# A decode-step kernel on one core: value products of two heads behind two transposes

## The chip, the cores and the metric

The kernel runs on one core of a Trainium2 chip. The metric is the device time of one execution in microseconds (us), lower is better. Engines are named as in the profile: PE (matrix products), PEld (PE's weight loads), DVE, ACT, POOL and SP; SP and POOL also issue DMAs.

## The reference, cut to what matters

One layer mixes two groups of heads over 512 prompt tokens and 32 sampled tokens: an RWKV-7 recurrence and a sparse attention with three branches (compressed, selected, sliding window). The change touches only the prompt's selected and window branches, which here are both full causal attention over the 512 tokens: a query may choose 16 blocks of 64 and there are only 8, and the window is 512 long.

```python
def masked_softmax(s, mask):
    s = jnp.where(mask, s.astype(jnp.float32), MASK_NEG)
    p = jax.nn.softmax(s, axis=-1)
    return jnp.where(mask, p, 0.0)

def window_attn(q, kw, qpos, kpos):
    mask = (kpos[None, :] <= qpos[:, None]) & (kpos[None, :] > qpos[:, None] - WINDOW) & (kpos[None, :] >= 0)
    s = jnp.einsum('bkgtd,bskd->bkgts', q, kw[:, :, 0]) * ATTN_SCALE
    p = masked_softmax(s, mask)
    return jnp.einsum('bkgts,bskd->bkgtd', p.astype(q.dtype), kw[:, :, 1])

# mixer_out: the three branches are weighted with sigmoid gates and added
    o = g[0] * o_c + g[1] * o_s + g[2] * o_w
```

There are 8 query heads, written as 4 groups g of 2 key/value heads k, each 64 wide.

## The kernel before, in words

The kernel has four stages: the input projection (to about 340 us), then the recurrence of the prompt interleaved with the prompt's attention (about 340 to 535 us), then the sampled tokens' attention over the paged cache together with the prompt's output projection, then a short end.

**The attention.** `attention()` goes through four token tiles i of 128 queries. For each tile it runs one unit `compressed(i)` and eight units `full(i, br, g)`, for 2 branches br and 4 groups g. A unit of `full` does, for both k: scores (L1231, L1232, and the causal mask L1233) into a PSUM bank of `SBANK`, the row maximum on DVE (L1234), the exponential with its sum on ACT (L1235) into `pr`; then the weights are scaled on DVE by gate over sum (L1237 to L1244). The weights lie with queries on partitions, so they are transposed on PE (L1250) into a bank of `PBANK`, two key tiles and both k at once, a *part* of up to four 128x128 transposes. The part is copied to the SBUF tile `ps` (L1252 on DVE or L114 on ACT), and the value products (L1256) add `VP` times `ps` into the accumulator bank `OT`. A value product has 64 output rows: k=0 fills partitions 0 to 63, k=1 fills 64 to 127. The trace shows each such fp32 product as two records of 128x64 weights.

**Banks.** PSUM has eight banks. `PBANK` is the single bank `bn[2]` (bn_3254 in the order of instructions) until the recurrence is over; then `bt[0]` (bt_67) is added. `SBANK` is `bn[0]`, `bn[1]`, and later also the two `ba` banks. `ps` has two buffers.

**What sets the order.** `attention()` is a generator. The first yields of a unit (the scores) run, then up to `BK_` = 2 yields of the unit before it (transposes, value products) come between. The recurrence's generator paces the whole: each of its steps yields a number, and the attention is advanced until its own yields add up to it. That is only the order in which the program states the instructions. The framework's scheduler then orders every engine's instructions itself from the dependences, and takes an instruction ahead of an earlier one that is not yet ready in its own estimate. Each engine executes its list in order. From the third stage on the order is kept as written.

Of the kernel before, what the change touches and what calls it, by code (L numbers as in the profile page):

```python
# [7 lines left out]
F32 = mybir.dt.float32  # L8
# [3 lines left out]
AF = mybir.ActivationFunctionType  # L12
OP = mybir.AluOpType
AX = mybir.AxisListType
PSUM = bass.MemoryType.PSUM

P = 128
# [30 lines left out]
PRE = 'dd'  # L48
# [10 lines left out]
def tile_hymba_step(  # L59
# [8 lines left out]
    nc = tc.nc  # L68
# [6 lines left out]
    small = ctx.enter_context(tc.tile_pool(name="small", bufs=4))  # L75
# [8 lines left out]
    def nxt(n, banks):  # L84
        turn[n] = (turn[n] + 1) % len(banks)
        return banks[turn[n]]
# [14 lines left out]
    mm = nc.tensor.matmul  # L101
    tp = nc.tensor.transpose
    act = nc.scalar.activation
    tt = nc.vector.tensor_tensor
    ts = nc.vector.tensor_scalar
    stt = nc.vector.scalar_tensor_tensor
    red = nc.vector.tensor_reduce
    cp = nc.vector.tensor_copy
# [4 lines left out]
    def acopy(o, i, scale=1.0):  # L113
        return act(o, i, AF.Copy, scale=scale)  # L114
# [8 lines left out]
    VP = vp.tile([P, 2, 4, P], F32, name="VP")  # L123
    gpt = vp.tile([P, 4, 24], F32, name="gpt")
# [83 lines left out]
    ident = ct([P, P], name="ident")  # L208
    ts(ident, jp, 0.0, None, op0=OP.is_equal)
    identb = ct([P, P], BF, name="identb")  # L210
    cp(identb, ident)
    causb = ct([P, P], BF, name="causb")
# [258 lines left out]
    for p in range(4):  # L471
# [49 lines left out]
        for c in range(NCH):  # L521
            tok = slice(c * C, c * C + C)
# [14 lines left out]
    for u in range(4):  # L537
        n = min(4, 13 - 4 * u)
# [25 lines left out]
    for s in range(31):  # L564
        n, m = s + 1, 31 - s
# [113 lines left out]
    qstk = QR.rearrange("p (k g n) -> p k g n", k=2, g=4)  # L679
    kdh = WR[:, 2048:4096].rearrange("p (b k n) -> p b k n", b=2, k=2)  # L680
    kdl = WR[:, 0:2048].rearrange("p (b k n) -> p b k n", b=2, k=2)
# [253 lines left out]
    at = pool(cs_, "at", 2)  # L935
# [245 lines left out]
    SBANK = [bn[0], bn[1]]  # L1181
    PBANK = [[bn[2], bt[1]], [bn[2]], [bn[2], bt[1]], [bn[2], bt[0]], [bn[2], bn[2], bt[0]]][NBK]
    OT = ob_.rearrange("p (g q) -> p g q", g=4)
# [33 lines left out]
                   skip_group_check=True)  # L1217
        yield 860

    def full(i, br, g):  # L1220


        n = (i + 1) * P
        nq = max(n, 256)
        tok = slice(i * P, n)
        l2 = small.tile([P, 2], F32, name="lb")
        nm = small.tile([P, 2], F32, name="nm")
        pr = at.tile([P, 2, NPR], F32, name="pr", bufs=NPRB)
        for k in range(2):
            S = nxt("s", SBANK)  # L1230
            mm(S[:, 0:nq], qstk[:, k, g, tok], kdh[:, br, k, 0:nq], start=True, stop=False)  # L1231
            mm(S[:, 0:nq], qstk[:, k, g, tok], kdl[:, br, k, 0:nq], start=False, stop=False)  # L1232
            mm(S[:, i * P:n], identb, causb, start=False, stop=True)  # L1233
            red(nm[:, k:k + 1], S[:, 0:n], axis=AX.X, op=OP.max, negate=True)  # L1234
            act(pr[:, k, 0:n], S[:, 0:n], AF.Exp, bias=nm[:, k:k + 1], accum_out=l2[:, k:k + 1])  # L1235
            yield 165 * (i + 1)
        nc.vector.reciprocal(l2, l2)  # L1237
        tt(l2, l2, gpt[:, i, 8 + 8 * br + g:16 + 8 * br:4], op=OP.mult)
        for k in range(2):
            e = PRE[k]  # L1240
            if e == "a":
                acopy(pr[:, k, 0:n], pr[:, k, 0:n], l2[:, k:k + 1])
            else:
                (nc.gpsimd if e == "p" else nc.vector).tensor_scalar(pr[:, k, 0:n], pr[:, k, 0:n], l2[:, k:k + 1], None, op0=OP.mult)  # L1244
        for t0 in range(0, i + 1, 2):
            nt = min(2, i + 1 - t0)
            pT = nxt("p", PBANK)
            for t in range(nt):
                for k in range(2):
                    tp(pT[:, (2 * t + k) * P:(2 * t + k + 1) * P], pr[:, k, (t0 + t) * P:(t0 + t + 1) * P], ident)  # L1250
            ps = at.tile([P, 512], F32, name="ps", bufs=2)
            (acopy if (g + t0 // 2) % 2 else cp)(ps[:, 0:2 * nt * P], pT[:, 0:2 * nt * P])  # L1252
            yield 220 * nt
            for t in range(nt):
                for k in range(2):
                    mm(OT[64 * k:64 * k + 64, g, :], VP[:, br, t0 + t, 64 * k:64 * k + 64],  # L1256
                       ps[:, (2 * t + k) * P:(2 * t + k + 1) * P], start=False,
                       stop=(br == 1 and t0 + t == i), skip_group_check=True)
            yield 150 * nt
        if g == 3 and br == 1:  # L1260
            tt(G[:, 4:8, tok], OT, G[:, 4:8, tok], op=OP.mult)

    def attention():
        units = []
        for i in range(4):
            units.append((compressed(i), 1))
            units += [(full(i, br, g), 2) for br in range(2) for g in range(4)]
        late, back = [], iter(())
        for u, n in units:
            for _ in range(n):  # L1270
                yield next(u)
                for _ in range(BK_):
                    y = next(back, None)
                    if y is not None:
                        yield y
            late.append(u)
            if len(late) > LAG:
                yield from back
                back = late.pop(0)
        for u in [back] + late:  # L1280
            yield from u

    A = attention()
    t = 0
    def side():
# [427 lines left out]
    with tc.manual_schedule(engines={ET.PE, ET.DVE, ET.Activation, ET.Pool}):  # L1713
        for s in range(8 * B):
            b, i = divmod(s, 8)
# [91 lines left out]
```

## Time and profile before

| what | us |
|---|---|
| median of 3 runs | 806.1 (802.2 to 810.11) |
| the profiled execution | 805.09 |
| its span (first to last instruction) | 803.3 |
| PE busy | 719.6 |
| DVE busy | 515.4 |
| ACT busy | 341.8 |
| value products, 320 records on PE | 27.4 |

Busy PE is not PE at its peak: a record's duration contains the time to drain, and the next product starts before it ends. What a product costs is read from the distance between starts.

### The profile page before, as it was taken

How to read it: one execution, taken by the hardware profiler on the slowest of the kernel's cores; microseconds unless marked ns; L12 is line 12 of the kernel's file. 1: busy time of each engine (PE TensorE's matmuls, PEld its weight loads, DVE VectorE, ACT ScalarE, POOL GpSimd, SP SyncE). 2: the span in 40 equal slices, each digit the busy share in tenths (PEclk: the TensorE clock that was granted, in tenths of full speed). 3: DMA queues.
4: the chain of work that ended last, by engine and by line, in shares of the span. 5: the costliest groups of instructions: out<-in, count | busy, mean ns of one | idle time of the engine just before them, and what ended most of it. 6: DMA issues, size and time to landing. Idle time of an engine off the chain costs nothing.

```text
span 803.3 us, 17119 instructions
## 1 busy us (share of the span) xinstructions
PE 719.6 (90%) x6922; PEld 602.2 (75%) x6922; DVE 515.4 (64%) x1236; ACT 341.8 (43%) x731; POOL 293.5 (37%) x323
## 2 busy tenths in 40 slices
PE   3997988998899999699999999988989999998775
PEld 2896977888787999598888787665757766676553
DVE  7687587779921520867766665855776666667653
ACT  5335635542021223234544343455554664656420
POOL 5276566554231164500011023224443554434100
PEclk9998998999799899769999999999999999999977
DMA  7733233265373133311115100389888889898841
GB/s 212 264 90 99 63 95 95 53 169 111 81 157 88 29 105 79 119 21 27 28 27 133 27 8 1 127 294 369 301 326 286 304 321 312 299 344 321 253 126 60
DMA packets 103912, 125.01 MB, mean 156 GB/s; under 512 B 59085, under 2 KB 90551, under 8 KB 95386
## 3 DMA queue, kind: packets, MB, share of 16 engines
q1 hardware_dynamic: 94074, 56.48, 26.4%
q0 software_dynamic: 9216, 67.11, 23.0%
q8 instruction: 54, 0.88, 0.4%
q10 hardware_dynamic: 544, 0.33, 0.2%
q14 instruction: 24, 0.20, 0.1%
HBM read 112.81 MB, written 15.26 MB: 159 GB/s over the span
## 4 chain that ended last, share of the span: by engine, by line
PE 61%; DVE 18%; DMA 10%; issue 5%; ACT 4%; POOL 2%; SPq 1%; POOLq 0%; DVEq 0%; ACTq 0%
PE bx L366 16%; DMA pg<-in_cache_kv_dram,idx 5%; PE bn L1256 2%; PE bn L1571 2%; PE ba L1391 2%; PE bt L1001 2%; PE bn L1250 2%; PE bt L1398 2%; PE bn L1519 2%; PE bn L1504 2%; PE bt L1009 1%; DVE LT L566 1%; PE bn L1231 1%; DVE CHL L1565 1%; PE bt L1381 1%
## 5 line engine op out<-in xcount | busy, mean ns | idle before, releaser
L366 PE MATMUL bx<-xh,WR 128*128 128x272 f32 x992 | 182.9, 300 | 2.6 <-POOL WR L360 2.3
L366 PEld LDWEIGHTS bx<-xh,WR 128*128 128x128 f32 x992 | 149.7, 197 | 6.2 <-POOL WR L360 2.7
L366 PE MATMUL bx<-xl,WR 128*128 128x272 f32 x496 | 110.5, 299 | 0.0
L1332 POOL DMA_INDIRECT pg<-in_cache_kv_dram,idx x64 | 62.6, 978 | 119.1 <-PE bn L1530 18.3
L360 POOL TENSOR_TENSOR WR<-WA,WR 128x1024 fp32r<-128x1024 f32 x31 | 76.1, 2454 | 70.5 <-ACT WR L114 70.3
L366 PEld LDWEIGHTS bx<-xl,WR 128*128 128x128 f32 x496 | 83.3, 198 | 0.9
L1571 PE MATMUL bn<-WHL,CHL 128*128 128x256 f32 x384 | 64.8, 304 | 3.9 <-DVE CHL L1565 2.6
L1571 PEld LDWEIGHTS bn<-WHL,CHL 128*128 128x128 f32 x384 | 51.7, 195 | 8.6 <-DVE CHL L1565 4.3
L114 ACT ACTIVATE WR<-WA 128x1024 fp32r<-128x1024 f32 x31 | 32.7, 1056 | 57.6 <-PE bx L366 26.7
L1382 DVE COPY ktc<-bt 128x512 f32<-128x512 f32 x38 | 26.1, 687 | 32.4 <-PE bt L1381 32.4
L1025 POOL TENSOR_TENSOR std<-st,DC 128x512 f32<-128x512 f32 x7 | 7.3, 1049 | 99.5 <-DVE st L1051 37.6
L1565 DVE TENSOR_TENSOR CHL<-G,CHL 128x256 fp32r<-128x256 f32 x64 | 32.2, 503 | 17.1 <-ACT CHL L114 17.1
L1235 ACT ACTIVATE pr<-bn,nm 128x128 f32<-128x128 f32 (+3 forms) x57 | 28.8, 507 | 26.1 <-PE bn L1250 12.1
L1391 PE MATMUL ba<-ktc,WA 128*32 128x255 f32 x512 | 34.0, 383 | 6.3 <-DVE ktc L1382 4.7
L114 ACT ACTIVATE kts<-bt 128x512 f32<-128x512 f32 x43 | 25.5, 593 | 31.1 <-PE bt L1398 31.1
L1234 DVE TENSOR_REDUCE nm<-bn 128x1 f32<-128x128 f32 (+3 forms) x57 | 26.0, 461 | 7.1 <-PE bn L1233 6.7
L1555 POOL TENSOR_TENSOR WHL<-WA,WHL 128x512 fp32r<-128x512 f32 x16 | 21.1, 1338 | 25.7 <-ACT WHL L114 25.7
L1398 PEld LDWEIGHTS bt<-ident,pg 128*128 128x128 f32 x172 | 18.6, 140 | 15.0 <-issue 10.0
L114 ACT ACTIVATE vt<-pg 128x1024 f32<-128x1024 f32 x28 | 29.4, 1048 | 0.0
L1398 PE MATMUL bt<-ident,pg 128*128 128x128 f32 x172 | 27.4, 282 | 2.1 <-DMA pg<-in_cache_kv_dram,idx 2.0
L1256 PE MATMUL bn<-ps,VP 128*64 128x128 f32 x320 | 27.4, 287 | 1.2 <-ACT ps L114 1.0
L1391 PEld LDWEIGHTS ba<-ktc,WA 128*32 128x32 f32 x512 | 14.3, 109 | 18.0 <-DVE ktc L1382 5.2
(544 smaller groups left out, 1774.7 us busy)
## 6 DMA issues: line engine op xcount, KB each, us to landing
WA<-in_w_in_dram SPq DMA_DIRECT2D x23, 512.0 KB
WA<-in_w_in_dram SPq DMA_DIRECT2D x16, 256.0 KB
vt<-in_cache_kv_win_dram SPq DMA_DIRECT2D x8, 512.0 KB
out_dram<-in_cache_kv_win_dram SPq DMA_DIRECT2D x8, 508.0 KB
bkd<-bkv SPq DMA_DIRECT2D x4, 816.0 KB
bd<-bkd SPq DMA_DIRECT2D x16, 192.0 KB
xt<-in_x_prompt_dram SPq DMA_DIRECT2D x4, 512.0 KB
WA<-in_w_out_dram SPq DMA_DIRECT2D x4, 512.0 KB
```

The lines of the kernel that those rows point to most:

```text
L114: return act(o, i, AF.Copy, scale=scale)
L360: ptt(lo[:, :, :n], src[:, :, :n], h[:, :, :n], op=OP.subtract)
L366: mm(z[:, u, 0:HT], w[:, t, :], x[u][:, t, :], start=first, stop=last)
L1234: red(nm[:, k:k + 1], S[:, 0:n], axis=AX.X, op=OP.max, negate=True)
L1235: act(pr[:, k, 0:n], S[:, 0:n], AF.Exp, bias=nm[:, k:k + 1], accum_out=l2[:, k:k + 1])
L1256: mm(OT[64 * k:64 * k + 64, g, :], VP[:, br, t0 + t, 64 * k:64 * k + 64], ps[:, (2 * t + k) * P:(2 * t + k + 1) * P], start=False, stop=(b ...
L1332: nc.gpsimd.indirect_dma_start(out=t, out_offset=None, in_=cache_rows, in_offset=bass.IndirectOffsetOnAxis(ap=idx[:, 2 * b + c_t:2 * b + c ...
L1382: (acopy if i == 3 and b else cp)(KCT[b, q][:, :, c_t, :], pt.rearrange("p (t c) -> p t c", t=4))
L1391: mm(SCB[r, 0:255], QW[:, 4 * q + t, m, :], kt[:, t].rearrange("p a c -> p (a c)")[:, m:m + 255], start=(q == 0 and t < 2), stop=(q == 3 a ...
L1398: tp(pt[:, t * P:(t + 1) * P], PG[b, i][:, t, 2, :], ident)
L1565: tt(CHL[c][:, 1], cat, CHL[c][:, 0], op=OP.subtract)
L1571: mm(YB[:, 0:256], CHL[c][:, x, t], WHL[:, w, 2 * c + t], start=(c + t + x + w == 0), stop=(c + t == 2 and w == 1))
```

## The change: what it does, and the diff

`full` now takes a tuple of groups `gs`. In the first two token tiles a unit handles two groups, (0, 1) or (2, 3); both lie in one `pr` buffer, 256 columns each. In the last two tiles a unit still has one group, which has two parts. In every tile the unit now states all its transposes and copies first and all its value products after them, with one yield for the products instead of one for each part. `ps` has four buffers instead of two. The engine of the copy is chosen by `u + t0 // 2` instead of `g + t0 // 2`. The number of arithmetic operations and their shapes stay as they were.

```diff
-    def full(i, br, g):
+    def full(i, br, gs):
...
+        for u, g in enumerate(gs):
...
+            w = slice(256 * u, 256 * u + n)
...
-        for t0 in range(0, i + 1, 2):
+        parts = [(u, t0) for u in range(len(gs)) for t0 in range(0, i + 1, 2)]
+        made = []
+        for u, t0 in parts:
             nt = min(2, i + 1 - t0)
             pT = nxt("p", PBANK)
             for t in range(nt):
                 for k in range(2):
-                    tp(pT[:, (2 * t + k) * P:(2 * t + k + 1) * P], pr[:, k, (t0 + t) * P:(t0 + t + 1) * P], ident)
-            ps = at.tile([P, 512], F32, name="ps", bufs=2)
-            (acopy if (g + t0 // 2) % 2 else cp)(ps[:, 0:2 * nt * P], pT[:, 0:2 * nt * P])
+                    c = 256 * u + (t0 + t) * P
+                    tp(pT[:, (2 * t + k) * P:(2 * t + k + 1) * P], pr[:, k, c:c + P], ident)
+            ps = at.tile([P, 512], F32, name="ps", bufs=4)
+            (acopy if (u + t0 // 2) % 2 else cp)(ps[:, 0:2 * nt * P], pT[:, 0:2 * nt * P])
+            made.append((ps, nt))
             yield 220 * nt
+        for (u, t0), (ps, nt) in zip(parts, made):
             for t in range(nt):
                 for k in range(2):
-                    mm(OT[64 * k:64 * k + 64, g, :], VP[:, br, t0 + t, 64 * k:64 * k + 64],
+                    mm(OT[64 * k:64 * k + 64, gs[u], :], VP[:, br, t0 + t, 64 * k:64 * k + 64],
                        ps[:, (2 * t + k) * P:(2 * t + k + 1) * P], start=False,
                        stop=(br == 1 and t0 + t == i), skip_group_check=True)
-            yield 150 * nt
-        if g == 3 and br == 1:
+        yield 150 * (i + 1) * len(gs)
+        if gs[-1] == 3 and br == 1:
...
-            units += [(full(i, br, g), 2) for br in range(2) for g in range(4)]
+            units += [(full(i, br, gs), 2 * len(gs)) for br in range(2)
+                      for gs in (((0, 1), (2, 3)) if i < 2 else ((0,), (1,), (2,), (3,)))]
```

How the lists of the engines change is shown at three places of PE. In the changed kernel the lines are later: scores L1234 to L1236, transposes L1256, value products L1264. Lines L1001 to L1056 are the recurrence, L1124 to L1154 the sampled tokens' window.

The first place is a unit of two groups in the second token tile. Before:

```order
L1256 MATMUL bn_3255<-ps,VP 64x128 x4
L1250 MATMUL bn_3254<-ident,pr 128x128
L1231 MATMUL bn_3253<-WR,QR 128x256
L1232 MATMUL bn_3253<-WR,QR 128x256
L1233 LDWEIGHTS identb
L1233 MATMUL bn_3253<-causb,identb 128x128
L1250 MATMUL bn_3254<-ident,pr 128x128 x3
```

Changed:

```order
L1256 MATMUL bn_3254<-ident,pr 128x128 x4
L1264 MATMUL bn_3255<-ps,VP 64x128 x4
L1039 MATMUL ba_70<-cw,fi_3312 128x128 x4
L1124 MATMUL bt_68<-ident,vt 128x128 x4
L1009 MATMUL bt_67<-ident,bd_3308 128x128 x4
L1264 MATMUL bn_3255<-ps,VP 64x128 x4
```

The value products of the two groups are stated next to each other in the program, and stand apart in PE's list, four and four, with twelve other products between them.

The second place is the end of the second token tile (bn_3255 is `OT`). Before, the four products stand together:

```order
L1009 MATMUL bt_67<-ident,bd_3307 128x128 x4
L1154 MATMUL bt_68<-ident,sw 32x128
L1256 MATMUL bn_3255<-ps,VP 64x128 x4
L1250 MATMUL bn_3254<-ident,pr 128x128 x4
L1231 MATMUL bn_3252<-WR,QR 128x384
```

Changed:

```order
L1264 MATMUL bn_3255<-ps,VP 64x128 x3
L1001 MATMUL bt_67<-AR,bd_3307 128x128 x4
L1264 MATMUL bn_3255<-ps,VP 64x128
L1234 MATMUL bn_3252<-WR,QR 128x384
L1021 MATMUL ba_69<-WA,tm_3310 128x128 x4
L1027 MATMUL ba_69<-AR,st 128x128 x4
L1149 MATMUL bt_68<-ident,sw 128x128 x4
L1264 MATMUL bn_3255<-ps,VP 64x128 x3
L1001 MATMUL bt_67<-AR,bd_3307 128x128 x4
L1264 MATMUL bn_3255<-ps,VP 64x128
L1235 MATMUL bn_3252<-WR,QR 128x384
```

Two runs of four are each broken into three and one by products of the recurrence. The same happens twice to the eight products of the compressed branch (L1216), into 3 and 5 and into 1, 2 and 5.

The third place is the end of the attention, after the last scores. Before:

```order
L1256 MATMUL bn_3255<-ps,VP 64x128 x4
L1250 MATMUL bt_67<-ident,pr 128x128 x4
L1256 MATMUL bn_3255<-ps,VP 64x128 x4
L1250 MATMUL bn_3254<-ident,pr 128x128 x8
L1256 MATMUL bn_3255<-ps,VP 64x128 x8
L1250 MATMUL bt_67<-ident,pr 128x128 x4
L1250 MATMUL bn_3254<-ident,pr 128x128
L1256 MATMUL bn_3255<-ps,VP 64x128 x8
```

Changed:

```order
L1264 MATMUL bn_3255<-ps,VP 64x128 x4
L1256 MATMUL bt_67<-ident,pr 128x128 x4
L1264 MATMUL bn_3255<-ps,VP 64x128 x4
L1256 MATMUL bn_3254<-ident,pr 128x128 x4
L1264 MATMUL bn_3255<-ps,VP 64x128 x4
L1256 MATMUL bt_67<-ident,pr 128x128 x4
L1264 MATMUL bn_3255<-ps,VP 64x128 x4
L1256 MATMUL bn_3254<-ident,pr 128x128 x4
L1264 MATMUL bn_3255<-ps,VP 64x128 x4
L1256 MATMUL bt_67<-ident,pr 128x128
L1264 MATMUL bn_3255<-ps,VP 64x128 x4
```

The transposes now alternate between the two banks, where before eight in a row went to one bank, and the runs of eight value products became runs of four.

## Rows read from the trace of the kernel before

**Rows 1.** Page: busy time, then 40 slices of the span in tenths.

```profile
PE 719.6 (90%) x6922; PEld 602.2 (75%) x6922; DVE 515.4 (64%) x1236; ACT 341.8 (43%) x731; POOL 293.5 (37%) x323
...
PE   3997988998899999699999999988989999998775
...
PEclk9998998999799899769999999999999999999977
```

**Rows 2.** Windows of the attention: length, busy us by engine, clock, DMA share, GB/s.

```profile
440.00:460.00 20.00, 19.78 (x201) 16.11 (x200) 12.85 (x37) 9.00 (x22) 1.05 (x1) 1.00 0.13 28
460.00:480.00 20.00, 20.00 (x173) 16.31 (x172) 12.83 (x30) 7.42 (x20) 5.22 (x4) 1.00 0.03 7
480.00:500.00 20.00, 19.65 (x179) 16.10 (x179) 13.78 (x35) 7.22 (x19) 7.75 (x8) 1.00 0.01 2
...
520.00:540.00 20.00, 16.61 (x169) 12.04 (x165) 12.40 (x28) 9.98 (x23) 3.71 (x3) 1.00 0.82 294
```

**Rows 3.** Waits of PE, 375 to 520 us: waited for, total, times, longest.

```profile
PE ba L1039 <- DVE cw L979: 0.3, 1, 0.3
PE ba L1231 <- ACT pr L1235: 0.3, 1, 0.3
PE bn L1256 <- ACT ps L114: 0.2, 1, 0.2
PE bn L1231 <- ACT pr L1235: 0.2, 1, 0.2
```

**Rows 4.** Timeline of PE, two stretches: start, duration, engine, line, records.

```profile
400.49 0.60 PE L1009 MATMUL bt<-ident,bd 128*128 128x128 f32 x4
400.92 0.60 PE L1124 MATMUL bt<-ident,vt 128*128 128x128 f32 x4
...
519.59 0.66 PE L1256 MATMUL bn<-ps,VP 128*64 128x128 f32 x8
520.18 0.66 PE L1250 MATMUL bn<-ident,pr 128*128 128x128 f32 x4
520.76 0.66 PE L1256 MATMUL bn<-ps,VP 128*64 128x128 f32 x8
...
528.28 0.66 PE L1250 MATMUL bn<-ident,pr 128*128 128x128 f32 x4 [0.85 <-DVE ps L1252]
528.96 1.09 PE L1256 MATMUL bn<-ps,VP 128*64 128x128 f32 x16
529.98 0.66 PE L1250 MATMUL bt<-ident,pr 128*128 128x128 f32 x4
```

**Rows 5.** Waits of PE, 500 to 600 us, those of the attention's end.

```profile
PE bn L1256 <- ACT ps L114: 1.0, 3, 0.4
PE bn L1250 <- DVE ps L1252: 0.9, 1, 0.9
PE bn L1381 <- DVE G L1261: 0.8, 1, 0.8
PE bn L1250 <- DVE pr L1244: 0.7, 1, 0.7
...
PE bn L1256 <- DVE ps L1252: 0.2, 1, 0.2
```

**Rows 6.** Tile ps, 340 to 540 us: ns min/median/max; the copies' idle time by releaser.

```profile
L1252 DVE COPY ps<-bn x20: 411/680/692, 355.0 to 533.9; 128x512 f32<-128x512 f32 x12, 128x256 f32<-128x256 f32 x8
L114 ACT ACTIVATE ps<-bn x20: 374/592/622, 357.2 to 530.1; 128x512 f32<-128x512 f32 x12, 128x256 f32<-128x256 f32 x8
...
  PE bn L1250: 16.8, 14
```

**Rows 7.** Chain that ended last, 520 to 545 us, in order of time.

```profile
526.01 1.16 ACT WHL L114 x2
...
530.00 6.84 DMA WA<-in_w_out_dram
...
540.14 7.41 DMA pg<-in_cache_kv_dram,idx
```

More of the change, by code (lines that the diff above doesn't have):

```diff
@@ L1225, in full @@
         tok = slice(i * P, n)
-        l2 = small.tile([P, 2], F32, name="lb")
-        nm = small.tile([P, 2], F32, name="nm")
         pr = at.tile([P, 2, NPR], F32, name="pr", bufs=NPRB)
[L1229 to L1244, printed above, removed]
-        for t0 in range(0, i + 1, 2):
+        for u, g in enumerate(gs):
+            l2 = small.tile([P, 2], F32, name="lb")
+            nm = small.tile([P, 2], F32, name="nm")
+            w = slice(256 * u, 256 * u + n)
+            for k in range(2):
+                S = nxt("s", SBANK)
+                mm(S[:, 0:nq], qstk[:, k, g, tok], kdh[:, br, k, 0:nq], start=True, stop=False)
+                mm(S[:, 0:nq], qstk[:, k, g, tok], kdl[:, br, k, 0:nq], start=False, stop=False)
+                mm(S[:, i * P:n], identb, causb, start=False, stop=True)
+                red(nm[:, k:k + 1], S[:, 0:n], axis=AX.X, op=OP.max, negate=True)
+                act(pr[:, k, w], S[:, 0:n], AF.Exp, bias=nm[:, k:k + 1], accum_out=l2[:, k:k + 1])
+                yield 165 * (i + 1)
+            nc.vector.reciprocal(l2, l2)
+            tt(l2, l2, gpt[:, i, 8 + 8 * br + g:16 + 8 * br:4], op=OP.mult)
+            for k in range(2):
+                e = PRE[k]
+                if e == "a":
+                    acopy(pr[:, k, w], pr[:, k, w], l2[:, k:k + 1])
+                else:
+                    (nc.gpsimd if e == "p" else nc.vector).tensor_scalar(pr[:, k, w], pr[:, k, w], l2[:, k:k + 1], None, op0=OP.mult)
```

## The prediction

> **What bounds the kernel now.** I read the page first. PE is busy 90% of the span, the next engine 64%, and in the slices where attention and recurrence run together PE shows a 9 nearly everywhere, at full granted clock [rows 1]. The windows say the same of the stage itself: between 440 and 500 us PE has at least 19.65 of every 20 us, DVE at most 13.8, ACT at most 9.0, and DMA hardly moves [rows 2]. A busy engine can still be waiting inside its list, so I read its waits next: from 375 to 520 us the four waits that are listed sum to 1.0 us of 145 [rows 3]. So this stage lasts as long as PE's list takes, with no other engine's work on its path, and a change of the list counts one for one, whether in products or in what lies between them. That holds to about 524 us. At the end of the attention PE does wait, 3.6 us in all [rows 5]: the recurrence is over, and transposes, copies and value products of the last heads follow one another with nothing else to put between them.
>
> **What a run of value products costs.** The change moves such runs, so their price is the main one. Eight records (four products) take 0.59 us from start to the next start (519.59 to 520.18), sixteen take 1.02 (528.96 to 529.98) [rows 4]. Eight records more thus cost 0.43, and a run of eight has 0.16 us beside its products. Four transpose records between ordinary products take 0.43 us (400.49 to 400.92); between two value runs they take 0.58 (520.18 to 520.76) [rows 4]. That is another 0.15. Going into the 64-column shape and back costs **0.31 us per run**, however long the run is. A second price follows: a transpose record takes 0.108 us, a value record 0.054, so the products of k=0 and k=1 run side by side. A product left without its partner should take the time of the pair, 0.22 us by my estimate from these rows.
>
> **The change, part by part.**
>
> *The runs.* As the program states them, the products of two parts come together. In tiles 0 and 1 that would be 8 runs instead of 16, in tiles 2 and 3 16 instead of 32. But PE's list is not the program's. The second part's transposes need the first part's bank emptied and its own weights scaled, and by then the first part's products are ready and are taken first. The three places shown say so, and over the whole stage PE's list has 45 runs of value products before and 47 now (16 of two products both times). Counting every step between full-width, 64- and 32-column shapes from the first scores to the last value product, there are 119 changes before and 127 now. Eight changes more are four runs' worth: 4 x 0.31 = **+1.2 us**.
>
> *Broken pairs.* Four runs are broken at an odd place: value runs 3+1 twice, the compressed branch 3+5 and 1+2+5. Each leaves one product more without partner: 4 x 0.22 = **+0.9 us**. The ends are 0 (if neighbours pair anyway) and 0.9; I take the upper one, since half the record time in [rows 4] can only come from pairing.
>
> *The second transposes on one bank.* Until the recurrence ends there is one bank for transposes. Transposes that directly follow others on the same bank wait 0.85 us for the copy [rows 4]; that is the upper end for each of the 24 second transposes of a unit, and 0 is the lower. I take 0: the list puts other work in between. In the first place shown, three fours of recurrence and window products, 3 x 0.43 = 1.3 us, pass before the second run, and DVE and ACT wait for these transposes, 16.8 us before 14 copies, much more than PE waits for them [rows 6, 3].
>
> *The copies' engines.* In tile 2 all wide copies (0.69 us) go to DVE and all narrow ones (0.37) to ACT; before, each engine had half. DVE gets four wide for four narrow: 4 x (0.69 - 0.41) = 1.1 us over some 60 us of which it is busy about 39 [rows 6, 2]. It is covered by PE. Tiles 0, 1 and 3 divide the copies as before. The two more `ps` buffers cost nothing on any engine; no wait for a free `ps` is among PE's [rows 3].
>
> *The end.* Before, eight transposes in a row go to one bank, and the second four wait 0.85 us. Now they alternate and that wait should go. Yet with runs of four instead of eight there is less work between a transpose and the products on its copy, and three such waits of at most 0.4 us each are there already [rows 5]. Two more at 0.3 give +0.6; net **-0.3 us**. The ends: all waits of PE there gone, -3.6; each of six runs waits 0.4 and nothing is won, +2.4. I stay near the middle because the list exchanges one kind of wait for the other.
>
> *Behind the attention.* The last score products let the output projection's first tiles be written (ACT at 526.01, then the load of 6.84 us on the path [rows 7]). They keep their place relative to the end of PE's list, and the issues of SP, and of POOL from the first page load on, stay in the same order. POOL puts four query products ahead of one step of the recurrence; POOL is busy under 8 of 20 us there [rows 2]. What the attention gains or loses is handed on one for one.
>
> **The sum.** +1.2 + 0.9 - 0.3 = +1.8 us on the profiled execution's 805.1 us, that is 806.9. The median of the runs is 1.0 above that execution, so 807.9 is what I expect of a median: **808 us**, no change that a measurement of this kernel can tell (that takes about 1%, 8 us).
>
> **The rivals.**
>
> 1. *The grouping works as stated* (24 runs instead of 45). For it: the program's text, and a price per run that is real. Against it: PE's list, which shows the runs apart. Price: 21 x 0.31 = 6.5 us, giving 806.1 - 6.5 = 799.6. Even this is under 1%. Chance 0.05.
>
> 2. *Slower: the one transposing bank becomes the bound.* Place: tiles 0 to 2 and the start of 3, bank bn_3254. All transposes of a unit must now pass it before the program states any product, so a late copy by DVE or ACT holds PE's list. Price: up to 24 x 0.85 = 20 us [rows 4], giving 826. It decides from the point where the work between two transposes on that bank falls under 0.85 us; the 1.3 us above speak against, DVE's higher load for it. Chance 0.08. The Trainium skill, page "TensorEngine Tiling (Array Packing)", section "PSUM Bottleneck", argues this way: tiling makes the products quicker but not the emptying of PSUM, so the copy may become the bottleneck. By that rule the time would come out near this rival's; the rows of before show the copies waiting for PE instead.
>
> 3. *The end loses its waits altogether*, since two banks and four `ps` buffers take turns: 807.9 + 0.3 - 3.6 = 804.6. For it: the alternation at the third place. Against: shorter runs. Chance 0.07.
>
> My forecast has 0.80.
>
> **Range and chances.** Three runs of before spread over 7.9 us, so a median can lie some 4 us off without any cause; with the ends of the two uncertain terms (-3.3 to +2.7 at the end, -0.9 for the pairs) the range is 801 to 814. That holds the forecast and rival 3 and leaves out rival 2 and half of rival 1. Faster by over 1% (under 798) needs rival 1 with luck: 0.04. Slower by over 1% (over 814.2) is rival 2 and a little scatter: 0.10. Within 1%: 0.86.
>
> **What would show it.** In the profile after, the value products must still stand in about 45 runs, with the same steps of 0.59 us per eight records; if they stand in 24, the list was misread. PE's waits between 375 and 520 us must stay at 1 to 2 us; if transposes (L1256) are listed there as waiting for `ps` copies with several us, rival 2 holds. The wait of 0.85 us on one bank at the end should be gone, and waits of value products for copies be more numerous. The stage's end, the last value product at about 535 us, should move by no more than 3 us. A time off by more than 8 us with these rows as forecast would mean that something outside the attention moved, which I have not looked for.

## The result, and the profile after

The changed kernel takes 809.4 us (median of 20 runs, 804.14 to 817.34), the kernel before 804.35 (median of 20, 799.15 to 810.11). The ratio leaves out the run of 817.34 us, in which the chip ran in a slower state: 1.0053, 95% interval [1.0033, 1.0073], +4.3 us. That is a loss of half a percent, real but under the 1% that I had called telling. The forecast was 808 and "within 1%". The sum behind it gave +1.8 us; so the sign was right and the loss more than twice as large as worked out. The profiled execution took 811.29 us, its span is 809.1.

The page of the profile, to be read beside [rows 1]: busy time, then the 40 slices.

```profile
PE 727.2 (90%) x6922; PEld 609.8 (75%) x6922; DVE 518.6 (64%) x1236; ACT 339.0 (42%) x731; POOL 292.4 (36%) x323
...
PE   3997988899899999699999999989889999998875
...
PEclk9998999989799899779999998999999999999978
```

PE has the same 6922 instructions and is busy 7.6 us longer. A slice is 20 us long; in the row of the clock the slice from 485 to 505 us (the fifth figure of the third ten, an 8) stood at 9 before, one figure among several that differ. The windows say it plainly, beside [rows 2] (length, busy us by engine, clock, DMA share, GB/s).

```profile
480.00:500.00 20.00, 19.80 (x156) 17.74 (x154) 9.34 (x26) 5.61 (x15) 8.06 (x9) 0.83 0.00 1
520.00:540.00 20.00, 17.67 (x151) 11.90 (x148) 15.09 (x33) 11.49 (x28) 6.68 (x6) 0.92 0.87 325
```

Both windows stood at a granted clock of 1.00 before. Now it is 0.83 and 0.92, with PE as busy as ever: in the first it gets through 156 records where it got through 179.

The waits of PE, 375 to 522 us, beside [rows 3] (us in total, times, longest).

```profile
PE bn L1264 <- DVE ps L1258: 0.4, 1, 0.4
PE ba L1234 <- ACT pr L1238: 0.3, 1, 0.3
PE bn L1256 <- DVE ps L1258: 0.2, 1, 0.2
```

They sum to 0.9 us; it was 1.0. Single waits came and went, the sum stayed. The transposes are now L1256, the value products L1264, the copies L1258 on DVE and L114 on ACT.

The timeline of PE, two stretches at full clock, beside [rows 4] (start, duration, engine, line, records; what a run costs is the distance to the next start).

```profile
400.07 0.66 PE L1264 MATMUL bn<-ps,VP 128*64 128x128 f32 x8
400.65 1.16 PE L1039 MATMUL ba<-cw,fi 128*128 128x128 f32 x8
...
412.67 0.65 PE L1264 MATMUL bn<-ps,VP 128*64 128x128 f32 x6
413.25 1.16 PE L1001 MATMUL bt<-AR,bd 128*128 128x128 f32 x8
414.34 0.43 PE L1264 MATMUL bn<-ps,VP 128*64 128x128 f32 x2
414.71 0.44 PE L1234 MATMUL bn<-WR,QR 128*128 128x384 f32 x1
```

Four products (8 records) cost 0.58 to 0.59, as before. Three products (6 records) cost 0.58 too, and one product alone 0.37. Over all 47 runs of value products in this trace, at full clock and without a wait behind them, the step is 0.36 for one product, 0.37 for two, 0.58 for three, 0.59 for four and 1.02 for eight: a product without partner takes the time of a pair.

The waits of the attention's end, 500 to 600 us, beside [rows 5], and PE's timeline there, with the window of a stretch at half clock.

```profile
PE bt L1256 <- DVE pr L1247: 1.6, 1, 1.6
...
PE bn L1264 <- DVE ps L1258: 1.1, 3, 0.5
PE bn L1390 <- DVE G L1269: 0.8, 1, 0.8
...
PE bn L1256 <- DVE ps L1258: 0.2, 1, 0.2
```

```profile
532.82 0.66 PE L1264 MATMUL bn<-ps,VP 128*64 128x128 f32 x8
535.09 0.94 PE L1256 MATMUL bt<-ident,pr 128*128 128x128 f32 x4 [1.61 <-DVE pr L1247]
535.96 0.66 PE L1264 MATMUL bn<-ps,VP 128*64 128x128 f32 x8
536.55 0.95 PE L1256 MATMUL bn<-ident,pr 128*128 128x128 f32 x4
537.43 1.12 PE L1264 MATMUL bn<-ps,VP 128*64 128x128 f32 x8
```

```profile
536.80:540.20 3.40, 3.40 (x22) 2.19 (x21) 1.07 (x4) 0.60 (x1) 0.00 (x0) 0.50 1.05 339
```

The 0.85 us for one bank [rows 4] are gone. In their place the transposes of a later head wait 1.61 us for the weights that DVE scales. Before, one wait of 0.7 us was for scaled weights [rows 5]. The sum is 3.7 us, against 3.6. And a new thing: from 536.8 on the clock is halved for 3.4 us (the window behind the timeline), and the same instructions take longer. Four value products take 1.05 us to the next start instead of 0.59 (537.43 to 538.48); four transposes, partly ahead of the fall, 0.88 instead of 0.59.

Tile `ps`, beside [rows 6] (ns min/median/max, first and last start; then the copies' idle time by what ended it, us and times).

```profile
L114 ACT ACTIVATE ps<-bn x24: 367/493/603, 357.8 to 541.1; 128x256 f32<-128x256 f32 x12, 128x512 f32<-128x512 f32 x12
L1258 DVE COPY ps<-bn x16: 415/681/692, 355.8 to 499.1; 128x512 f32<-128x512 f32 x12, 128x256 f32<-128x256 f32 x4
L1258 DVE COPY ps<-bt x8: 673/692/692, 513.5 to 540.7; 128x512 f32<-128x512 f32 x8
...
  PE bn L1256: 10.4, 8
  PE bt L1256: 3.8, 4
```

DVE has 20 wide copies and 4 narrow ones instead of the even shares of before; each takes what it took. DVE and ACT still wait for the transposes, 14.2 us before 12 copies. The chain that ended last, beside [rows 7]:

```profile
541.48 1.12 PE bn L1264 x16
542.62 0.70 DVE G L1269
...
557.98 8.16 DMA pg<-in_cache_kv_dram,idx
```

It now runs through the last value products and the gating behind them (G). Before, it was on ACT by 526.01, for the output projection's tiles, and ran from there over a load. The attention's last product has come to lie on the path. That is so in all three profiles of the change, but also in the kernel below that loses nothing (the copies' engines as before), so it is not by itself the loss.

### The profile page after: what moved, and what is told of

It is laid out like the page before. It is cut to its first block, busy times and chain, and to the rows that moved or that the text cites. A ratio compares the mean times of both kernels' runs of the same rounds, so it can differ in the third digit from the quotient of the medians.

```text
span 809.1 us, 17120 instructions
## 1 busy us (share of the span) xinstructions
PE 727.2 (90%) x6922; PEld 609.8 (75%) x6922; DVE 518.6 (64%) x1236; ACT 339.0 (42%) x731; POOL 292.4 (36%) x323
## 4 chain that ended last, share of the span: by engine, by line
PE 63%; DVE 18%; DMA 8%; issue 5%; ACT 3%; POOL 2%; SPq 0%; POOLq 0%; DVEq 0%; ACTq 0%
PE bx L366 16%; DMA pg<-in_cache_kv_dram,idx 4%; PE bn L1580 3%; PE bn L1264 3%; PE ba L1400 3%; PE bt L1001 2%; PE bt L1407 2%; PE bn L1256 2%; PE bn L1513 2%; PE bt L1009 2%; DVE LT L566 2%; PE bn L1528 2%; PE bt L1390 2%; PE bn L1234 1%; DVE CHL L1574 1%
## 5 line engine op out<-in xcount | busy, mean ns | idle before, releaser
L366 PE MATMUL bx<-xh,WR 128*128 128x272 f32 x992 | 184.7, 303 | 3.2 <-POOL WR L360 2.3
L366 PEld LDWEIGHTS bx<-xh,WR 128*128 128x128 f32 x992 | 151.4, 199 | 6.8 <-POOL WR L360 2.8
L366 PE MATMUL bx<-xl,WR 128*128 128x272 f32 x496 | 111.4, 301 | 0.0
L366 PEld LDWEIGHTS bx<-xl,WR 128*128 128x128 f32 x496 | 84.3, 200 | 0.9
L114 ACT ACTIVATE WR<-WA 128x1024 fp32r<-128x1024 f32 x31 | 32.7, 1056 | 57.9 <-PE bx L366 26.9
L114 ACT ACTIVATE kts<-bt 128x512 f32<-128x512 f32 x43 | 25.5, 592 | 33.0 <-PE bt L1407 29.2
L1264 PE MATMUL bn<-ps,VP 128*64 128x128 f32 x320 | 29.1, 294 | 1.1 <-DVE ps L1258 1.1
L1564 POOL TENSOR_TENSOR WHL<-WA,WHL 128x512 fp32r<-128x512 f32 x16 | 20.9, 1331 | 24.5 <-ACT WHL L114 24.5
L114 ACT ACTIVATE vt<-pg 128x1024 f32<-128x1024 f32 x28 | 29.4, 1049 | 0.0
```

The lines of the kernel that those rows point to most:

```text
L366: mm(z[:, u, 0:HT], w[:, t, :], x[u][:, t, :], start=first, stop=last)
L1264: mm(OT[64 * k:64 * k + 64, gs[u], :], VP[:, br, t0 + t, 64 * k:64 * k + 64], ps[:, (2 * t + k) * P:(2 * t + k + 1) * P], start=False, sto ...
```

## The experiments

One number is compared throughout: the **stage**, from the end of the last input projection product (L366) to the end of the last value product. **Half-clock time** is the time within it at a granted clock of 1.2 GHz; the rest is at 2.4 GHz. "Steps" are the changes between products of full width, 64 and 32 columns in PE's list, "lone" the products without partner, both counted as for the prediction. The column "sum" is what the prices of the prediction (0.155 us per step, 0.22 per lone product) and half of the half-clock time give against the kernel before; for the key sums issued twice it has 0.9 us more for the added products. Each row but the repeated ones rests on one profile. Each ratio is to the kernel before, run beside it.

| kernel | steps | lone | half-clock us | stage us | against before | sum | ratio of the runs |
|---|---|---|---|---|---|---|---|
| before | 119 | 0 | 23.9 | 208.9 | | | 1 |
| before, second profile | 119 | 0 | 23.9 | 208.8 | -0.1 | 0 | 1.0003 |
| change | 127 | 4 | 30.7 | 214.5 | +5.6 | +5.5 | 1.0053 |
| change, second profile | 127 | 4 | 30.7 | 214.5 | +5.6 | +5.5 | 1.0077 |
| change, third profile | 127 | 4 | 23.9 | 211.2 | +2.3 | +2.1 | 1.0046 |
| one call of key sums wide | 127 | 4 | 23.9 | 211.3 | +2.4 | +2.1 | 1.0043 |
| all key sums wide | 130 | 3 | 13.7 | 206.9 | -2.0 | -2.7 | 0.9981 |
| copies' engines as before | 125 | 4 | 20.5 | 209.4 | +0.5 | +0.1 | 0.9999 |
| the same, key sums twice | 125 | 4 | 23.9 | 213.1 | +4.2 | +2.7 | 1.0033 |
| two-head units alone | 122 | 2 | 27.3 | 210.4 | +1.5 | +2.6 | 1.0015 |
| late products alone | 115 | 0 | 23.9 | 208.9 | 0.0 | -0.6 | 1.0010 |
| reversed products | 79 | 1 | 30.7 | 208.0 | -0.9 | -2.6 | 0.9993 |
| before, key sums wide | 121 | 1 | 20.5 | 208.8 | -0.1 | -1.2 | 0.9985 |
| reversed, key sums wide | 90 | 2 | 17.1 | 204.6 | -4.3 | -7.5 | 0.9951 |

### The change again

No edit.

> The changed kernel once more, with a second profile. If the half-clock stretch near 486 to 492 us of its first profile (about 6.8 us at 1.2 GHz, absent before) belongs to its order of products, it is there again and the ratio is about 1.005. If it was chance of one execution, it is gone from this profile; the ratio of the runs then still has to be explained by the price list alone (+2.1 us, 1.0026).

1.0077 [1.0053, 1.0101]. The profile has the stage of the first to 0.1 us, and the clock falls at the same place of the list, at 481.1 us, 153.6 us after the fall at the stage's start in both (windows; the stretch at half clock is the whole window).

```profile
481.10:487.90 6.80, 6.80 (x34) 6.80 (x34) 3.19 (x11) 1.01 (x2) 1.64 (x1) 0.50 0.00 0
```

So the fall was no accident of one profile. That it is no fixture either came out later (below).

### Products in reversed order of the parts

```diff
-        for (u, t0), (ps, nt) in zip(parts, made):
+        for (u, t0), (ps, nt) in reversed(list(zip(parts, made))):
...
-                       stop=(br == 1 and t0 + t == i), skip_group_check=True)
+                       stop=(br == 1 and t0 == 0 and t == nt - 1), skip_group_check=True)
```

> The changed kernel with the value products of a unit stated in reverse, last part first, so that the first of them waits for the last copy and PE's list cannot split them: 26 runs of value products instead of 45, 79 changes of shape instead of 119. Theory 'price list' (each pair of shape changes costs 0.31 us, each lone product 0.22 us): 40 changes fewer are -6.2 us, one lone product +0.2, so about 6 us faster than before, ratio 0.9925. Rival 'one bank' (transposes must wait for copies): PE's waits between 375 and 520 us grow to over 5 us and the gain is eaten, ratio 0.998 or more. Rival 'clock only' (the order matters only through the granted clock): ratio near 1 unless a half-clock stretch comes or goes.

0.9993 [0.9967, 1.0018]: the expected 0.9925 is outside the interval. The products of a unit add into one accumulator in the order stated. With the last part's stated first, none of them can go ahead of the last copy, and PE's list does group them: 79 steps instead of 127. The stage is 6.5 us shorter than that of the change (first two profiles) at the same half-clock time. The prices give 48 x 0.155 + 3 x 0.22 = 8.1. Some 1.6 us are lost again, 0.9 of it in waits: between 345 and 545 us PE's listed waits sum to 5.3 us, against 4.4 in the change and in the kernel before. Grouping pays when the list does it, at some four fifths of the price read from the rows of before. Against the kernel before it is no measurable gain: three stretches at half clock (3.4 us each) stand in its profile, and the 6.8 us of half-clock time that it has beyond the kernel before take some 3.4 us, by the half, of what the order wins.

### Late products alone

The change with single-head units in all tiles, and the copies' engines of before.

```diff
-                      for gs in (((0, 1), (2, 3)) if i < 2 else ((0,), (1,), (2,), (3,)))]
+                      for gs in ((0,), (1,), (2,), (3,))]
...
-            (acopy if (u + t0 // 2) % 2 else cp)(ps[:, 0:2 * nt * P], pT[:, 0:2 * nt * P])
+            (acopy if (gs[u] + t0 // 2) % 2 else cp)(ps[:, 0:2 * nt * P], pT[:, 0:2 * nt * P])
```

> Only the second half of the change: units of one head in all tiles, all transposes of a unit stated ahead of its value products, four buffers of ps, the copy's engine chosen as before. 44 runs of value products, 115 changes of shape, no lone product. Price list: 4 changes fewer, -0.6 us, ratio 0.999. If stating the products later costs by itself (one bank), ratio 1.005 like the whole change.

1.001 [0.9989, 1.0032], a stage of 208.9 with before's half-clock time. The rival's 1.005 is outside the interval: stating the products behind all copies does nothing by itself that could be measured.

### Two-head units alone

Each part's products are stated behind its own transposes again, with before's copies' engines; the units of two heads stay.

```diff
-            (acopy if (u + t0 // 2) % 2 else cp)(ps[:, 0:2 * nt * P], pT[:, 0:2 * nt * P])
-            made.append((ps, nt))
+            (acopy if (gs[u] + t0 // 2) % 2 else cp)(ps[:, 0:2 * nt * P], pT[:, 0:2 * nt * P])
...
-        for (u, t0), (ps, nt) in zip(parts, made):
...
-        yield 150 * (i + 1) * len(gs)
+            yield 150 * nt
```

> One part of the change alone: units of two groups in the first two token tiles, but each part's value products are stated right behind its transposes, and its copies' engines are those of before. 122 steps, 2 lone products: +0.5 and +0.4, +0.9 us by the list, a ratio of 1.001. Theory A: with the change's half-clock stretches 1.0055, without them 1.001. Theory C (the loss comes from stating the products behind all copies): 1.000.

1.0015 [0.9983, 1.0046]: not told apart from the expected 1.001, nor from 1. The stage is 1.1 us shorter than the sum says; why, the runs don't show.

### All key sums wide

The key sums of the normalisation (L1073) move 2 columns in the change; here 128. The first call of the five stands in the half-clock stretch at the start of the stage, the fourth at 485 us.

```diff
-            mm(v[:n, 2 * p:2 * p + 2], y2[:, p, :], bo[:, 0:P:64], start=True, stop=True)
+            mm(v[:n, p * P:(p + 1) * P], y2[:, p, :], bo, start=True, stop=True)
...
-        ts(rs[:n], v[:n, 0:8], 1.0 / 64, 64e-5, op0=OP.mult, op1=OP.add)
+        ts(rs[:n], v[:n, 0:512:64], 1.0 / 64, 64e-5, op0=OP.mult, op1=OP.add)
```

> The changed kernel in which the recurrence's sums of squares (L1073) stream 128 columns instead of 2 and use the same two of them; their weight loads take as long as before. The scheduler reorders other products too: 51 runs of value products, 130 changes of shape, three lone products. Price list alone: 11 changes more than before, +1.7, and +0.7, so +2.4 us, ratio 1.003. Theory 'clock': the half-clock stretch after the compressed scores of the last tile goes, some 3.4 us less than the changed kernel has, ratio 1.000 to 1.002.

0.9981 [0.9955, 1.0007], under both forecasts, and about 5.8 us faster than the change by its 1.0053, though the list has three steps more. The half-clock time falls by 17.0 us, from 30.7 to 13.7; half of that is 8.5, and the stage is 7.6 us shorter. Windows at the start of the stage (one stretch of 20.5 us in the change):

```profile
328.10:334.90 6.80, 4.50 (x17) 3.26 (x17) 6.64 (x39) 1.15 (x5) 1.58 (x5) 0.50 0.52 197
334.90:338.30 3.40, 2.50 (x25) 2.36 (x24) 2.72 (x21) 0.85 (x4) 1.67 (x1) 1.00 0.13 40
338.30:345.10 6.80, 6.80 (x43) 6.05 (x44) 4.45 (x13) 0.97 (x4) 0.63 (x2) 0.50 0.00 1
```

The full clock comes back for 3.4 us in between, and for good 21.0 us after the stage's start instead of 24.5. This was the first sign that the clock was the missing term.

### The kernel before, key sums wide

The same edit on the kernel before.

> The kernel before, with the key-sum products (L1073) 128 columns wide instead of 2; nothing else is edited. 121 steps against 119, 1 lone product against 0: +0.5 us by the list. Theory A (half-clock time counts half of its length): the 23.9 us at 1.2 GHz at the start of the stage become some 13.7, -5.1 us, so -4.6 in all, a ratio of 0.994. Theory B (the clock is not what the wide sums changed): +0.5 us or a little more for the wider products, 1.001 to 1.003.

0.9985 [0.9955, 1.0015]: the expected 0.994 is outside the interval. The start of the stage did get its 10 us at full clock back, but two stretches of 3.4 us appeared elsewhere (413.9 and 485.6 us), and the wide sums have a small price that I had left out. The first call, timeline of this kernel:

```profile
335.99 1.92 PE L1073 MATMUL bt<-bo,AR 128*32 128x128 f32 x8
337.83 0.58 PE L1231 MATMUL bn<-WR,QR 128*128 128x256 f32 x1
```

Its step is 1.84 us at 1.2 GHz; with 2 columns it was 1.42, a 0.83 us wait included. Of the 0.42 us more, 0.25 come back in PE's next wait, for the tile `kc`, 0.35 us instead of 0.60; the other four calls take up to 0.1 us more each. The half-clock time of the whole stage fell by 3.4 us only, not by 10: while it went in one place, it appeared in others. That the one brought the other is not shown.

### Reversed products, key sums wide

Both edits on the change.

> Two edits of the change together: the value products are stated in the reverse order of their parts, and the key-sum products of the recurrence's normalisation (L1073) have 128 moving columns instead of 2. PE's list has 90 steps between shapes and 2 lone products. Theory A (the price per step, 0.155 us, the lone product, 0.22 us, and half of the time spent at a granted clock of 1.2 GHz): -29 steps x 0.155 = -4.5, +0.4, and if the half-clock time falls from 23.9 us in the kernel before to about 13.7, as it did with the wide key sums alone, -5.1: some -9 us, a ratio of 0.989. Theory B (steps alone, the clock stretches lie beside the matter): -4.1 us, 0.995. Theory C (the change's loss comes from waits for copies, and grouping brings more of them): 1.000 or above, as with the reversed order alone.

0.9951 [0.9921, 0.9981], 800.68 us against 803.37: the only version here that measurably beats both kernels. Theory A's 0.989 is outside the interval; the number is the 0.995 of theory B, by which the clock doesn't matter. The stage, 4.3 us shorter, is a little over half of what the sum gives. Of the missing 3.2 us, 1.7 stand in its waits, 6.1 us between 345 and 545 us against 4.4, and some 0.5 in the wide sums (above); about 1 us stays open. With the same 2.2 us added, theory B's sum would give -1.9, further off than the -5.3 of theory A, so the stage doesn't speak for B. The waits, in the timeline of the attention's end:

```profile
525.55 1.09 PE L1264 MATMUL bn<-ps,VP 128*64 128x128 f32 x16 [1.91 <-ACT ps L114]
...
531.60 1.10 PE L1264 MATMUL bn<-ps,VP 128*64 128x128 f32 x16 [0.73 <-ACT ps L114]
```

The eight products of one run wait for a copy by ACT, 1.91 and 0.73 us, and in PE's list nothing stands at this place that could run meanwhile.

### The copies' engines as before

```diff
-            (acopy if (u + t0 // 2) % 2 else cp)(ps[:, 0:2 * nt * P], pT[:, 0:2 * nt * P])
+            (acopy if (gs[u] + t0 // 2) % 2 else cp)(ps[:, 0:2 * nt * P], pT[:, 0:2 * nt * P])
```

> The change with the copies' engines chosen by the group's number, as before the change, instead of by the place in the unit. 125 steps, 4 lone products: +0.9 and +0.9, +1.8 us by the list. Theory A: if the list then keeps the key sums of the last tiles directly behind the 32-column products, the two half-clock stretches of the change remain (+3.4 us), 1.0065; if it does not, they go, and 1.002 is left. Theory C (DVE's load in tile 2 made the change slower): 1.000 to 1.001 with the clock as in the change.

0.9999 [0.997, 1.0028]: the loss is gone with this one line. By itself that would point at DVE's load. The profile says otherwise: PE's waits for copies between 345 and 520 us are 0.3 us here and 0.6 in the change, and all its listed waits to 545 us are 4.9 here and 4.4 there, so the copies have nothing to give back. PE's list differs with the line, but little, by two steps (0.3 us). What differs more is the clock: neither the stretch at 485 us nor that at 537 us is there, 20.5 us of half-clock time against 30.7, and the stage is 5.1 us shorter, which is half of the difference (PE's timeline of this kernel at the place in question; then, from its waits, the longest, which ends at 530.1 us).

```profile
484.84 1.03 PE L1073 MATMUL bt<-bo,AR 128*128 128x2 f32 x8
485.74 0.63 PE L1009 MATMUL bt<-ident,bd 128*128 128x128 f32 x4
...
487.11 1.16 PE L1045 MATMUL ba<-tm 128*128 128x128 f32 x8
```

```profile
PE bn L1256 <- DVE ps L1258: 2.1, 1, 2.1
```

My expectation of the place was wrong: the 2-column products stand directly behind the 32-column ones here too, at full clock. That they are neighbours doesn't decide.

### The same, with the key sums of 485 us twice

```diff
-        for p in range(4):
+        for p in list(range(4)) * (2 if t.start == 256 else 1):
```

> The kernel that differs from the change in its copies' engines and lost nothing (0.9999), with the same four 2-column products at 485 us issued twice. Its list has them directly behind the 32-column products too, yet its profile showed 2.4 GHz there. Theory A, if it is the length of the narrow work in one piece that lets the clock fall: the four records more take 0.9 us, and a stretch of 3.4 to 6.8 us at 1.2 GHz appears behind them: +0.9 and +1.7 to +3.4, a ratio of 1.003 to 1.005. If the clock stays: +0.9 us, 1.001.

1.0033 [1.0005, 1.0062]. In the profile the clock now falls behind them (timeline, with 12 of the 16 records in the first row, then the window of the stretch):

```profile
483.78 1.48 PE L1073 MATMUL bt<-bo,AR 128*128 128x2 f32 x12
485.12 0.64 PE L1009 MATMUL bt<-ident,bd 128*128 128x128 f32 x4
...
486.49 2.01 PE L1045 MATMUL ba<-tm 128*128 128x128 f32 x8
```

```profile
486.60:490.00 3.40, 3.40 (x17) 3.40 (x18) 0.01 (x1) 0.06 (x1) 0.70 (x1) 0.50 0.00 0
```

The stretch came, as one branch of the expectation had it, with a stage 3.7 us longer: 0.9 for the products, 1.7 for the stretch, 1.1 not accounted for. With one profile of each kernel, taken on different chips, this doesn't settle that the added products brought the fall. The 12 runs of each say a little more. Over the whole execution the half-clock time (reckoned as in the last part of this section) is 1.6 us above that of the kernel before beside it, and without the added products 6.3 us below: a difference of 7.8 us (2.7 to 13.0), which goes with the edit, though the runs don't say where in the execution it lies.

### The change a third time, and one call of key sums wide

The first is the change unedited; the second edits exactly one row of PE's list, the key sums at 485 us (128 columns instead of 2), by the edit shown above under the condition `t.start == 256`.

> The change as it is, beside the other two kernels of this comparison. All theories: 1.0053 to 1.0077 as in the two comparisons before, and in the profile a stretch of about 6.8 us at 1.2 GHz some 153 us after the one at the stage's start.

> The change with one row of PE's list edited: the key sums of the third pair of chunks (four products, at 485 us in the change's profile, directly behind the 32-column products) have 128 moving columns instead of 2. All else in the list is as in the change: 127 steps, 4 lone products, the same copies' engines. Theory A (half-clock time is the term that was missing): the stretch of 6.83 us at 485 us goes, -3.4 us or more, a ratio of 1.001 to 1.003 to the kernel before, and the rest of the loss (steps and lone products, about +2) stays. Theory B (the change loses by its own products, waits or copies, and the clock stretch lies beside it): 1.005 to 1.008, as the change.

1.0046 [1.0021, 1.007] and 1.0043 [1.0019, 1.0066]: no measurable difference. The 1.0043 lies between the two forecasts, and its interval reaches both, so this run decides for neither; and since the unedited change beside it shows no fall at the place either, its profile says nothing about the row. But the unedited change gave the best evidence of all, by accident. Its third profile shows no fall at that place. PE's timeline there in the first profile of the change, and in the third:

```profile
485.32 1.64 PE L1073 MATMUL bt<-bo,AR 128*128 128x2 f32 x8
486.82 1.09 PE L1009 MATMUL bt<-ident,bd 128*128 128x128 f32 x4
487.71 1.06 PE L1256 MATMUL bn<-ident,pr 128*128 128x128 f32 x4
488.56 1.91 PE L1045 MATMUL ba<-tm 128*128 128x128 f32 x8
490.27 1.92 PE L1047 MATMUL ba<-cw,tm 128*128 128x128 f32 x8
```

```profile
482.83 1.03 PE L1073 MATMUL bt<-bo,AR 128*128 128x2 f32 x8
483.72 0.63 PE L1009 MATMUL bt<-ident,bd 128*128 128x128 f32 x4
484.19 0.60 PE L1256 MATMUL bn<-ident,pr 128*128 128x128 f32 x4
484.63 1.06 PE L1045 MATMUL ba<-tm 128*128 128x128 f32 x8
485.52 1.06 PE L1047 MATMUL ba<-cw,tm 128*128 128x128 f32 x8
```

Same program, same list. From the key sums to the end of L1047's step the first takes 6.66 us (485.32 to the next start, 491.98), the second 3.58 (482.83 to 486.41). The windows say why:

```profile
485.60:492.40 6.80, 6.80 (x34) 6.80 (x33) 3.17 (x11) 1.01 (x2) 1.64 (x1) 0.50 0.00 0
```

```profile
482.80:489.60 6.80, 6.80 (x67) 6.23 (x68) 4.80 (x15) 2.06 (x5) 4.41 (x6) 1.00 0.00 0
```

PE is busy all the time in both, with 34 records at half clock and 67 at full. The stage without the stretch is 3.3 us shorter, half of 6.8. So the clock term is shown by itself, with nothing edited; and whether the clock falls at this place varies from one execution to another. The second and the third profile were taken on different chips, so that the chip decides is not excluded; three profiles can't tell.

### The kernel before a second time

> The kernel before, looked at a second time, since three profiles of the change gave two stages of 214.5 us and one of 211.2 with one and the same list. Theory A (the list of before takes about 209 us, and every us at 1.2 GHz beyond the 23.9 of its first profile adds half a us): a stage of 208.9 plus half of the difference in half-clock time, whatever that is. Theory B (the stage varies by itself, and the clock stretches lie beside it): the stage differs by more than 0.5 us from that.

1.0003 [0.9959, 1.0046]. Stage 208.8 us, half-clock time 23.9 in one stretch at the start: the first profile over again. Since the half-clock time was the same, theory A's half was not put to the test; what it shows is that two profiles with the same half-clock time agree to 0.1 us, against theory B.

### All runs together

Each run, profiled or timed, comes with its span and mean granted clock; 2 x (1 - clock) x span is its half-clock time over the whole execution. In 35 runs of the change it is 95.9 us on average, in 89 runs of the kernel before 90.2. Over 230 runs of the kernels of the table (without those taken with the second profile of before), each kernel with its own base, an us of half-clock time goes with 0.29 us of span (0.25 to 0.33). That is less than the half seen in the stage. Outside it the halved clock also falls where PE is idle for part of the time (in the kernel before, from 760 us to the end of the span, PE is busy 26.4 of 43.3 us at a clock of 0.83); that this is the reason is not shown. The loss of the change in these runs is 808.7 - 803.7 = 5.0 us. Of it the list has 2.1 (the sum of steps and lone products), the waits of the end 0.1, the clock 5.7 x 0.29 to 5.7 x 0.5 = 1.6 to 2.9, and 0.3 to 0.4 lie outside the span: device time less span is 2.2 us in the change and 1.8 in the kernel before. I have no cause for the last. One kernel warns against giving the clock more than that: with one call of key sums wide, the half-clock time is 90.6 us, that of the kernel before beside it 90.8, and the loss is still 3.4 us on average. The list and the time outside the span (2.1 + 0.4) leave 0.9 us of it open.

## Why the prediction was right, and where it was not

- *PE's list counts one for one.* Right. No wait came in (0.9 us in the middle of the stage), and the third profile's stage grew by 2.3 us where the list's prices give 2.1.
- *The grouping is not in PE's list.* Right: 47 runs of value products in the trace, as read from the order of instructions. When the list does group (reversed products), 6.5 us of the change's stage come back, so rival 1 was a real price on a condition that didn't hold.
- *Price of a run and of a broken pair, +1.2 and +0.9.* Right to some tenths; three products cost what four do, one what two do.
- *One transposing bank, the copies' engines, +0.* Right for the waits. Transposes waited 0.2 us for copies in the middle of the stage; rival 2 (826 us) is out. But the choice of the copies' engines was not free: with that line put back the loss is gone, not through a wait, but with a shorter half-clock time. The Trainium skill, page "TensorEngine Tiling (Array Packing)", section "PSUM Bottleneck", warned of the copies; the trace does not agree here, DVE and ACT still wait for PE (14.2 us before 12 copies).
- *The end, -0.3.* The size was near, partly by luck. The one-bank wait of 0.85 went, as forecast. What came for it was not what was forecast, more waits of value products for copies (1.1 us now, 1.2 before), but a longer wait of transposes for scaled weights, 1.6 us instead of 0.7; net +0.1. Rival 3 (all waits gone) is out. But in all three profiles of the change the clock fell for 3.4 us in this end, at 531 to 537 us. It costs 1.7 us, half of its length, and was in no term.
- *Behind the attention, one for one.* Nothing speaks against it, though the path moved onto the attention's last product. From the stage's end to the end of the span it is 267.9 and 264.9 us in the two profiles of before, 266.5, 265.1 and 268.7 in the three of the change.
- *What failed: "at full granted clock" as a constant.* I read the clock of before in the attention (1.00 in every window of [rows 2]) and carried it over to a list in another order. So the sum lacked a term altogether: +3.4 us of stage in the first two profiles (half of 6.8 more), nothing in the third, where the 3.4 us of the end are balanced by a stretch at the stage's start that is 3.4 us shorter than before, and an estimated 1.6 to 2.9 on average over the runs. The sign that I had set for it was missed: the last value product was to move by no more than 3 us, and in the first profile it ended at 542.6 us instead of 535.3; 5.6 of these 7.2 us lie within the stage.
- *The base.* I added to 805.1 and the median of three runs, 806.1. With 20 runs that median is 804.35. A base 1.75 too high and a loss some 3 us too small offset each other in part, so it is luck that 808 lies as near to 809.4 as it does.

The Trainium skill, page "TensorE: Matmul & The Clock Gate", section "HAM oscillation — how this bites in real kernels", reckons the penalty of throttled time at half of it. The stage agrees (6.8 us of it, 3.3 us of stage). The section tells of throttling that follows PE's idle gaps. That is not what stands at 485 us, where PE shows no listed wait ahead of the fall and is busy throughout. At the stage's end a wait does stand ahead of the fall, the 1.61 us that end 1.7 us before it; yet the kernel with the copies' engines as before waits 2.1 us there, and its clock doesn't fall in the rest of the stage. What PE did before the fall at 485 us was narrow: 32-column scores, then 2-column sums. Since the same list also ran through at full clock, what decides is open.

## What to carry to other kernels

Count the runs in the engine's own list, not in the program: a scheduler that takes what is ready can split what the program groups; here stating the last-ready part first, so that the others depend on it, held most of a group together. Price a switch and a broken pair from distances between starts; in the changed kernel both held to a few tenths. And when instructions move on a bound PE, treat the granted clock as a term with its own range: read it by stretch in more than one profile of the same kernel, before crediting or blaming an edit that only moved the clock.

## What the runs showed of the hardware that I had not expected

- The clock fell to 1.2 GHz in the middle of a stretch in which PE was 100% busy and no wait is listed: 6.8 us at 0.50 in two of three profiles of one program, 1.00 in the third, which was taken on another chip than the second.
- An fp32 product of 64 output rows costs the same alone as with its partner on the other column half: 0.36 against 0.37 us for the run, 0.58 for three and 0.59 for four.
- Four key-sum products of 2 moving columns and of 128 take nearly the same at full clock, in one place of the list: steps of 0.89 (482.83 to 483.72) and 0.97 us (483.07 to 484.04, in the kernel with one wide call).
